# A new table of turns for a hybrid decoder layer: the same instructions in another order on every engine

## The chip, the cores and the metric

The kernel runs on one core of one Trainium2 chip. The core has a matrix engine (TensorE, PE in the profile; its weight loads are shown apart, as PEld), a vector engine (VectorE, DVE), an engine for activation functions (ScalarE, ACT), a general one (GpSimd, POOL), and SyncE (SP), whose queue issues the transfers between memory and SBUF. Each engine carries out its instructions in the order in which they stand in its queue, and engines wait for one another by semaphores. The metric is the time of one execution in microseconds of device time, as the median over runs. The kernel before took 839.03 us (three runs, 837.23 to 841.96).

## The reference

One layer of a decoder with 1024 tokens of width 1024, all in fp32. Cut to its steps:

```python
h = rms_norm(x, attn_norm_w)
a_q, a_k, a_v, a_z, a_b, a_a, b_q, b_k, b_v, b_z, i_q, i_k, i_w = split(h @ w_in)
# A: gated DeltaNet, 4 heads of 128, in chunks
qkv = silu(causal_dwconv(concat(a_q, a_k, a_v), conv_w))        # 4 taps
o_a = rms_norm(gated_delta_rule_chunked(q, k, v, g, beta)) * silu(a_z)
#   per chunk: v_new = val - kcd @ S; o = qd @ S + att @ v_new; S = S * gl + kd^T @ v_new
# B: sparse attention, 8 heads of 64 over 2 heads of keys and values
score = sum_h i_w[h] * relu(i_q[h] . i_k)                       # indexer, causal
o_b = softmax(b_q . b_k over the 256 keys of highest score) @ b_v * silu(b_z)
x = x + concat(o_a, o_b) @ w_out
x = x + (p @ w_ple) * sigmoid(rms_norm(x) @ w_gate + b_gate)
```

## The kernel before, in words

Tokens or channels lie on the 128 partitions, and matrices are worked in tiles of 128 x 512. An fp32 product is made of three matmuls in the type fp32r: each weight tile `raww` is loaded, rounded on ACT to `hiw` (L578), and the rest `low` is formed on POOL (L580); PE then multiplies high by high, low by high and high by low (`mm3`, L754). There are two buffers for `raww` and four each for `hiw` and `low`, so a weight tile's load waits until POOL has done with the one two before.

The work in rough order: RMSNorm, the per-layer embedding product (`start`, L772, with `pled` written out to memory for later); the indexer's products and scores (`logits`, L1047); the projections of four DeltaNet heads, each with a convolution of three taps on DVE (`tap`, L1237, which writes `acc` and `accq`); the inverse of a triangular matrix per chunk (`ftmp`, `Ub`, `Bb`); the recurrence (`gdn_s2`, L1358); the search for the 256th score of each row; attention; the output product; and the gate stage at the end.

The recurrence of one head has eight chunks. In each, PE multiplies the state S (into `rec`), DVE makes r from it, PE multiplies r by U, DVE makes `vnew`, PE multiplies `vnew` by `kh`, and DVE makes the next S from that. Other work of PE fills the time between these steps. Heads are counted from 0.

The search for the threshold is a bisection. For the last three blocks of 128 rows it runs on ACT (`junka` counts) and POOL (`nt`, `upa`), and ends with `va`. Then `topk_mask` (L1071) masks each block's row in two pieces on DVE: compare (`eq`), running count (`cum`), and two more passes, after which ACT writes the mask into `score`. The attention's keys `kst`, values `vst` and queries `Qt` are loaded into buffers that lie where the search's were (L1734 to L1750); ACT and DVE split Qt into the high and low part `qT`. PE makes the score products `S` from `kst` and `qT`.

In the gate stage (L1954 on) an output tile goes through: product on PE, DVE's scaling (`gth<-mm,rb`), ACT's sigmoid, DVE's product with the embedding (`gth<-gth,pld`), the sum with x, and the transfer out. `pld` has two buffers, `gth` two, and the tiles of the second half of the tokens are eight, the last of them cut into two pieces of 256 columns.

All engine calls are first recorded, 7513 of them with the marks of buffers, and each knows what it depends on. `Plan.run` (L457) then unpacks the text `TURNS` (L75) into one order of all records and `Plan.issue` (L506) issues them in it; an engine's queue holds its own calls in that order. Since L526 issues everything, every row of the profile has this line, and one reads it by the names of the tiles. A transfer, too, has its place in SP's queue by this table.

Of the kernel before, what the change touches and what calls it, by code (L numbers as in the profile page):

```python
# [2062 lines left out]
```

## Time and profile before

| | |
|---|---|
| runs | 837.23, 839.03, 841.96 us; median 839.03 |
| profiled execution | 838.3 us, span 836.6 us, mean granted clock of PE 0.995 |
| PE busy | 822.1 us, 98% of the span, 5171 matmuls |
| PEld, DVE, ACT, POOL busy | 698.3, 600.2, 562.1, 484.5 us |
| DMA | 97.34 MB at a mean of 116 GB/s |

The span is the time from the first to the last instruction of one profiled execution; some time lies around it. An engine row of the timeline has start, duration, engine, line, operation, the tile written and those read, their shapes, the count of instructions that are put together in it and, in brackets, how long the engine stood idle before and what ended that. SPq is the issuing of transfers. A transfer's row tells when it was issued, and its landing is seen in who waited for it.

### The profile page before, as it was taken

How to read it: one execution, taken by the hardware profiler on the slowest of the kernel's cores; microseconds unless marked ns; L12 is line 12 of the kernel's file. 1: busy time of each engine (PE TensorE's matmuls, PEld its weight loads, DVE VectorE, ACT ScalarE, POOL GpSimd, SP SyncE). 2: the span in 40 equal slices, each digit the busy share in tenths (PEclk: the TensorE clock that was granted, in tenths of full speed). 3: DMA queues.
4: the chain of work that ended last, by engine and by line, in shares of the span. 5: the costliest groups of instructions: out<-in, count | busy, mean ns of one | idle time of the engine just before them, and what ended most of it. 6: DMA issues, size and time to landing. Idle time of an engine off the chain costs nothing.

```text
span 836.6 us, 14789 instructions
## 1 busy us (share of the span) xinstructions
PE 822.1 (98%) x5171; PEld 698.3 (83%) x5171; DVE 600.2 (72%) x1369; ACT 562.1 (67%) x1285; POOL 484.5 (58%) x652
## 2 busy tenths in 40 slices
PE   8999999999999999989999999999999999999997
PEld 6898889988888888878888888777888888888876
DVE  3672536669488988899999978697776778452645
ACT  6663565555559889968999974688765767555432
POOL 3443433242159386775667786467864667768861
PEclk9999999999999999999999999999999999999999
DMA  8953221311212232222223223547435331345454
GB/s 291 372 182 118 65 76 51 83 64 45 78 40 64 52 100 69 70 70 93 78 56 83 85 97 126 180 161 240 153 99 157 96 101 39 126 161 190 124 180 139
DMA packets 80171, 97.34 MB, mean 116 GB/s; under 512 B 24256, under 2 KB 40928, under 8 KB 79968
## 3 DMA queue, kind: packets, MB, share of 16 engines
q1 hardware_dynamic: 80096, 96.40, 36.0%
q8 instruction: 40, 0.66, 0.3%
q14 instruction: 35, 0.29, 0.1%
HBM read 70.92 MB, written 25.45 MB: 115 GB/s over the span
## 4 chain that ended last, share of the span: by engine, by line
PE 82%; DVE 7%; DMA 6%; ACT 2%; issue 1%; POOL 1%; SPq 1%; DVEq 0%; POOLq 0%; ACTq 0%
PE mm L526 57%; PE s L526 6%; PE lg L526 6%; PE S L526 3%; PE pv L526 3%; PE pt L526 3%; PE rec L526 2%; PE po L526 2%; DVE eq L526 1%; DMA xt<-in_x_dram 1%; DVE gth L526 1%; SPq L526 1%; DVE P L526 1%; DMA raww<-in_w_ple_dram 1%; DMA dN<-NB 1%
## 5 line engine op out<-in xcount | busy, mean ns | idle before, releaser
L526 POOL TENSOR_TENSOR low<-raww,hiw 128x512 fp32r<-128x512 f32 (+1 forms) x135 | 183.4, 1365 | 166.3 <-ACT hiw L526 149.1
L526 PE MATMUL mm<-hTlo,hiw 128*128 128x512 f32 (+1 forms) x528 | 198.5, 386 | 0.0
L526 PE MATMUL mm<-hThi,hiw 128*128 128x512 f32 (+1 forms) x528 | 197.1, 385 | 0.0
L526 PE MATMUL mm<-hThi,low 128*128 128x512 f32 (+1 forms) x528 | 196.8, 386 | 0.0
L526 ACT ACTIVATE hiw<-raww 128x512 fp32r<-128x512 f32 x133 | 82.8, 627 | 69.5 <-PE mm L526 23.2
L526 PEld LDWEIGHTS mm<-hThi,low 128*128 128x128 f32 x528 | 99.8, 190 | 16.3
L526 PEld LDWEIGHTS mm<-hTlo,hiw 128*128 128x128 f32 x528 | 99.4, 189 | 16.0
L526 PEld LDWEIGHTS mm<-hThi,hiw 128*128 128x128 f32 x528 | 99.3, 189 | 15.6
L526 ACT ACTIVATE junka<-score,nt 128x768 bf16<-128x768 int16 (+5 forms) x96 | 99.8, 1040 | 3.8 <-POOL nt L526 1.3
L526 POOL TENSOR_SCALAR P<-P,rsum 128x128 f32<-128x128 f32 (+7 forms) x64 | 50.4, 798 | 41.9 <-DVE rsum L526 37.1
L526 ACT ACTIVATE relu<-lg 128x384 f32<-128x384 f32 (+3 forms) x80 | 40.4, 523 | 48.4 <-PE lg L526 42.4
L526 DVE TENSOR_SCALAR_CACHE_REDUCE junk<-score,cand 128x384 bf16<-128x384 f32 (+2 forms) x96 | 71.1, 740 | 1.5
L526 DVE SCALAR_TENSOR_TENSOR score<-relu,sm,score 128x384 f32<-128x384 f32 (+5 forms) x42 | 43.6, 1046 | 20.8 <-ACT relu L526 19.9
L526 ACT ACTIVATE ph<-pt 128x512 fp32r<-128x512 f32 x72 | 41.0, 594 | 24.7 <-PE pt L526 22.7
L526 ACT ACTIVATE P<-P,mn 128x128 f32<-128x128 f32 (+7 forms) x64 | 49.3, 771 | 12.0 <-DVE mn L526 10.7
L526 POOL TENSOR_SCALAR nt<-acca,upa 128x1 f32<-128x1 f32 x96 | 37.5, 393 | 33.1 <-ACT junka L526 30.2
L526 PE MATMUL S<-kst,qT 128*128 128x384 f32 (+4 forms) x192 | 53.8, 354 | 2.2 <-DMA kst<-kd 1.9
L526 DVE TENSOR_TENSOR pl<-pt,ph 128x512 fp32r<-128x512 f32 x72 | 47.8, 685 | 10.9 <-ACT ph L526 10.4
L526 PE MATMUL mm<-mcl,hiw 128*128 128x512 f32 x128 | 49.4, 396 | 0.0
L526 DVE SCALAR_TENSOR_TENSOR acc<-fst,cw,acc 128x512 f32<-128x512 f32 x48 | 38.7, 808 | 14.6 <-ACT acc L526 13.5
L526 PE MATMUL mm<-mch,hiw 128*128 128x512 f32 x128 | 49.1, 397 | 0.0
L526 PE MATMUL mm<-mch,low 128*128 128x512 f32 x128 | 48.9, 394 | 0.0
(296 smaller groups left out, 2066.4 us busy)
## 6 DMA issues: line engine op xcount, KB each, us to landing
raww<-in_w_ct_dram SPq DMA_DIRECT2D x66, 256.0 KB, 3.1
raww<-in_w_out_dram SPq DMA_DIRECT2D x32, 256.0 KB, 3.1
raww<-in_w_gate_dram SPq DMA_DIRECT2D x32, 256.0 KB, 2.5
xt<-in_x_dram SPq DMA_DIRECT2D x8, 512.0 KB, 8.2
...
```

The costliest lines, as they stand in the source:

```text
L526: r = getattr(getattr(self.nc, o.eng), fn)(*[real(x) for x in args], **{k: real(v) for k, v in kw.items()})
```

## The change

The text `TURNS` is replaced by another of the same length in records. No call, tile, pool or dependence is changed, and every engine issues the same instructions. The 5171 matmuls of PE are 3981 records (some hold several small ones), and 3545 of these have another place (10.6 places away in the mean, 236 at most); on DVE 983 of 1174 have (4.9 in the mean), on ACT 873 of 1015 (5.2), on POOL 547 of 648 (4.9), and of the transfers on SP 291 of 394 (3.2, at most 60). The diff is 68 lines of packed text, whose rows tell a reader nothing, so one stands for all:

```diff
 TURNS = r"""
-c-rlG32;=`neJV?@9n$yU3%X)^&+XImRei4b_t;s2@oIwTF`2-*nrI<_8lRx*@BIU4H)s_g&1suA;w|K#*UrXabA+CdP&M}GMUV
...
+c-rlm2XqzpmH(&DyqPyMZ|3#ht6tGl?*d7v_ksjM6d@!;FOsn77R8ic0mcSlFrpgA!3Kgc7~Eomo!DO68#}hMiIWq@$!0hFeg2!
...
 """
```

The first place is the step from chunk 3 to chunk 4 in the recurrence of head 1. On PE, before, from the product of `vnew` with `kh` to the next product with S (buffer numbers follow the names):

```order
L526 MATMUL rec_2474<-vnew_2565,kh_2459 128x128
L526 MATMUL po_2564<-S_2581,accq_2404 128x128
L526 MATMUL po_2564<-vnew_2454,att_2572 128x128
L526 MATMUL po_2564<-S_2455,accq_2404 128x128
L526 MATMUL s_926<-accq_849,acc_0_865 128x128
L526 MATMUL s_955<-ident_104,accq_849 128x128
L526 MATMUL po_2564<-vnew_2565,att_2572 128x128
L526 MATMUL rec_2474<-S_2570,acc_0_1297 128x128
```

and now, from the same product on:

```order
L526 MATMUL rec_2461<-vnew_2618,kh_2465 128x128
L526 MATMUL mm_148<-hTlo_248,hiw_145 128x512
L526 MATMUL mm_143<-hThi_244,hiw_125 128x512
L526 MATMUL mm_143<-hTlo_248,hiw_125 128x512
L526 MATMUL mm_143<-hThi_244,low_144 128x512
L526 MATMUL mm_148<-hThi_244,low_154 128x512
```

Rows of this kind, of 512 columns, go on up to `rec<-S,acc`, which is the 42nd row behind the first one here; before, it was the seventh. On DVE, before, the last taps of the convolution, two steps of the inverse's sums, and S:

```order
L526 SCALAR_TENSOR_TENSOR acc_0_840<-fst_225,cw_528,acc_0_840 128x512 x3
L526 TENSOR_TENSOR ftmp_841<-Ub_1087,Bb_1086 128x8x12
L526 SCALAR_TENSOR_TENSOR acc_0_840<-fst_224,cw_528,acc_0_840 128x512 x2
L526 TENSOR_REDUCE Ub_1087<-ftmp_841 128x8
L526 TENSOR_TENSOR ftmp_841<-Ub_1087,Bb_1086 128x8x13
L526 SCALAR_TENSOR_TENSOR S_2570<-S_2455,egl_842,rec_2474 128x128
L526 TENSOR_REDUCE Ub_1087<-ftmp_841 128x8
```

and now, from the `vnew` of that step to S:

```order
L526 TENSOR_SCALAR vnew_2618<-rec_2461,br_2598 128x128
L526 SCALAR_TENSOR_TENSOR acc_0_841<-fst_115,cw_684,acc_0_841 128x512
L526 SCALAR_TENSOR_TENSOR acc_0_841<-fst_114,cw_684,acc_0_841 128x512
L526 SCALAR_TENSOR_TENSOR acc_0_841<-fst_115,cw_684,acc_0_841 128x512
L526 TENSOR_TENSOR att_1379<-s_1064,scr_861 128x512
L526 SCALAR_TENSOR_TENSOR acc_0_841<-fst_114,cw_684,acc_0_841 128x512
L526 TENSOR_SCALAR junk_2407,acc_2408<-score_947,cand_0_2629 128x384
L526 SCALAR_TENSOR_TENSOR acc_0_841<-fst_114,cw_684,acc_0_841 128x512
L526 SCALAR_TENSOR_TENSOR acc_0_841<-fst_115,cw_684,acc_0_841 128x512
L526 SCALAR_TENSOR_TENSOR S_2621<-S_2433,egl_768,rec_2461 128x128
```

The taps (`acc<-fst,cw,acc`) stand ahead of S in both; the inverse's sums (`ftmp`, `Ub`) now come behind S.

The second place is the end of the recurrence of head 3 and the first loads of the attention. On DVE, before, from the last r of head 3 through its last `vnew` into the masks of the fourth to last piece:

```order
L526 SCALAR_TENSOR_TENSOR r_2571<-rec_2474,neg_eg_924,v_2607 128x128
L526 TENSOR_SCALAR vnew_2565<-rec_2474,br_2586 128x128
L526 TENSOR_SCALAR eq_2625<-score_927,va_2631 128x448
L526 SCALAR_TENSOR_TENSOR cum_2407<-eq_2625 128x448
L526 SCALAR_TENSOR_TENSOR eq_2625<-cum_2407,neda_2731,eq_2625 128x448
L526 SCALAR_TENSOR_TENSOR eq_2625<-score_927,va_2631,eq_2625 128x448
L526 SCALAR_TENSOR_TENSOR z_2614<-s_926,wa_213,z_2614 128x512
```

and now, from the `vnew` of the last chunk but two to the last one:

```order
L526 TENSOR_SCALAR vnew_2618<-rec_2461,br_2598 128x128
L526 TENSOR_SCALAR eq_2668<-score_947,va_2672 128x448
L526 SCALAR_TENSOR_TENSOR S_2623<-S_2621,egl_768,rec_2461 128x128
L526 SCALAR_TENSOR_TENSOR z_2652<-s_1057,wa_80,z_2652 128x512
L526 SCALAR_TENSOR_TENSOR r_2434<-rec_2461,neg_eg_778,v_2650 128x128
L526 TENSOR_SCALAR vnew_2432<-rec_2461,br_2598 128x128
L526 SCALAR_TENSOR_TENSOR cum_2381<-eq_2668 128x448
L526 SCALAR_TENSOR_TENSOR S_2433<-S_2623,egl_768,rec_2461 128x128
L526 SCALAR_TENSOR_TENSOR eq_2668<-cum_2381,neda_2850,eq_2668 128x448
L526 SCALAR_TENSOR_TENSOR r_2622<-rec_2461,neg_eg_778,v_2650 128x128
L526 SCALAR_TENSOR_TENSOR eq_2668<-score_947,va_2672,eq_2668 128x448
L526 TENSOR_SCALAR vnew_2618<-rec_2461,br_2598 128x128
```

The first piece with 448 columns and one z are now done between the steps of the recurrence. On SP, the transfers of the attention before:

```order
L526 DMA mixd<-z_2582 128x512
L526 DMA mixd<-z_2614 128x512
L526 DMA Qt_5438<-qd 128x4x128
L526 DMA raww_114<-in_w_ct_dram 128x512
L526 DMA Qt_5437<-qd 128x4x128
L526 DMA kst_5432<-kd 128x4x128 x2
L526 DMA vst_5574<-vd 128x2048
```

and now:

```order
L526 DMA mixd<-z_2624 128x512
L526 DMA mixd<-z_2652 128x512
L526 DMA kst_5443<-kd 128x4x128
L526 DMA raww_122<-in_w_ct_dram 128x512
L526 DMA Qt_5463<-qd 128x4x128
L526 DMA kst_5443<-kd 128x4x128 x2
L526 DMA Qt_5464<-qd 128x4x128
```

The first load of `kst` now stands ahead of both loads of `Qt`, and a load of weights stands between `kst` and the first `Qt`.

The third place is the end of SP's queue, in the gate stage. Before (the last four pairs of gate weights are rows of `raww`, an output is `out_dram`):

```order
L526 DMA out_dram<-gth_5933 128x512
L526 DMA raww_115<-in_w_gate_dram 128x512
L526 DMA raww_114<-in_w_gate_dram 128x512
L526 DMA out_dram<-gth_5841 128x512
L526 DMA raww_115<-in_w_gate_dram 128x512
L526 DMA pld_5929<-pled 128x512
L526 DMA pld_5908<-pled 128x512
L526 DMA out_dram<-gth_5933 128x512
L526 DMA pld_5929<-pled 128x512
```

and now:

```order
L526 DMA out_dram<-gth_5899 128x512
L526 DMA pld_5886<-pled 128x512
L526 DMA raww_124<-in_w_gate_dram 128x512
L526 DMA raww_122<-in_w_gate_dram 128x512
L526 DMA pld_5889<-pled 128x512
L526 DMA out_dram<-gth_5882 128x512
L526 DMA raww_124<-in_w_gate_dram 128x512
L526 DMA raww_122<-in_w_gate_dram 128x512
L526 DMA pld_5886<-pled 128x512
L526 DMA out_dram<-gth_5899 128x512
L526 DMA raww_124<-in_w_gate_dram 128x512
L526 DMA pld_5889<-pled 128x512
```

The load of `pld` for the sixth output tile was the sixth row of the first of these pieces, behind three tiles of weights; it is the fifth of the second, ahead of the last three tiles of weights. An output and a `pld` load now stand ahead of each pair of weights.

More of the change, by code (lines that the diff above doesn't have):

```diff
@@ new lines @@
+5|ah+*E8U%%gb?{5$!yPzsuU0YoEP9E|ZX|Z3OKAja$Lu$|nUK6TBklJbG<w#muvbDOj93AY$iJJbSQ;#%vk@WbH;#XbyX=%B+NRIMuTYKOR5<!KsWH3-tf(K*
+%rAwD8m*WAr8VLsBd5_0~MBMIBDCBmxMFL@8Q(Jo{g0^+Ioo+YW^m}{?fk2U~9<O&e;nL(4p98TY@w8}KM8TF8EeYFW;cyt6Z*@2vsoHIRz;3t0D`j?Pfx}T;>
+?<nrISL92y!rVKm%|bDWoG((PG@?;>5e)4hzap}-Tukfyk4(TTO|+*Ih`)Vg_dabML>>Gk09ElF3Xaz=+o29W^*JGO*0z|dc7O-$}XpK+BB^J(E810z19fm3@M
+Tdru1~9F>XjR6bCSWp&o`pAJA*Pm?oL-iMydO>Cv?KeX_w|17y8k))_y;YPITQs4fQo91gu*!DKR7EEc_9z}*;+VYr~t*d{S+OeR?pL{U_W$t0g1z|_2gz^gTP
+0B=jONkLM6YPDXY(XG)qolZ&8eugaRQ2L>V5EaY8>l~;49EM@asfvmUhEXxZfnnkRMQJFC;wc5@PAH0$WtmhkHP2NoB}tYg$=i2l&*uIW24f@D(l*RavV3q6qb
@@ new lines @@
+ez(qhuOD<^hptin3&Kib_RMvBE-?O63aYD3ES<e}6wg(_Bms1mmzW92<eq^y%Tyz4sbbg82B-_3y?~#F_uAriDIQcvmQgl^9AL!r@|33>FlmmT)jDD>pYcFHcM
+)vV(z4h3%7M4xQK`R7Y12ZLd;jXlS@SuvV+n+0d{AaJ%bV?x4q8nZmPa)27XvH}6z1!7OX6T{9fZN;*1I%mzw&gjut6=1_ipV^>k#QElJCg$vt!z7;E0NVI_<2
+w{&)SGx<tFyB4v?gK1orobs8gB9n@nR5?N@VI#P?1c*#F8#V^xToj*`HO4UuHD#kuIC$1J@wSZix)4!BDiqjo8SB<Z_VQV5hhVq>!s`0t%I+<X8ZZiPoL%&DGU
+t_jf{-&1IK}(iFYQ>o;~~0*%K$uoC$@lUmqGCdcyPi>#u(Rwx$dQp$hTOUBccu^YYs-zx?u>Z@%%t2Ooa;;Ts=)H1D(uXP=I;PM7nIx88co>2kdxy*54$r|-Qt
+{_gi*{qVaVFcS0VTW`Jp{^ea`FYf)m=7A5nPd<6;moL5ak|clY+rn!P0Y7?3b-=*vH*dLk3Fa6~Lx1JX8#g}rME*AXRDHHcKYHbrSI#|u?%efrH_yHQ{`)s>d<
@@ new lines @@
+Xb|B%!3Y-xdDlUxdGU=e_r?zWe;mn>U%Yp6sUm)DC(Wd+O>nwVJ#6?2QYrTz&SVn?HPR<ds*hU%htz{4+1VeC31Zo_q1d=U#XL_j7{RD?I+xlaF6K$LY@VyjFN
+j;mVtDzImQF`Xm73ZMELGapS3zXH}2gIH6ElsnT3ObM4GG&YU^%_=!^|E}uDb>C)A!S5H3r=){SMXP$ZH`t|F_uU$KS9G;!{`-#8%yGxgU31=t&_HS?9I(eb#{
+P~IFPd<71^5t(ldf|zQW9QF*_?uIwPED{!`yOE*gQ;ZMlSjtKF@}+j7*D7T8V#7ON@8pWcaA-D>C#xAV6|@DwslWl-sl6{_Uzg7;)`(DHhOK8VIG;7m^iiM<o!
+Q7!92Z5*eF2#>+ieo*s){x{ndsyH^2S%+wX1Ix^?S@gGQ6V!-vEB){lgT4yYd8{nMZB-nVaP{n*fzE7#ZU8M=CPX!ovt?*K5_9}W-icxHIyYpktz-n>=8mBGaF
+<y*IY{p%}MtXi>h<yo*jI5}}*c;(8~t52*|SiXGu;lpcI+;h+J;o%2YuG}}i=8@H_S6;bt<<P{lYgVpWLDS2ZE`8uZnq53PN{fkwLOgzQ!GilI1_l=N4-Am~M;
@@ new lines @@
+9D9GO=+ZsK>hAfq{G056oY?Y=}EPHg<W{(?tJS@^5CJ>7Bg?>}jdOwrvzeE9@T~-8*_enA&^~rKr(IKisfo!-fs*?d>h=M^o%->*~5+VK>my(qgqnS2O}Umn=~
+<1kN^ZhVj`+?%2`N(r~o7xuId(wi74X+S(dgK>!-Y$HyC5zq$6|3ym#}jZICB`|sJeZy(4W*|NH>d1qbS;lqa;TAQ0kYlw{-vAwnHH*Ffw>#g2|USBp9$4g6{C
+Afl|mj|w@Ksn9I%Brm$1hQ(fva++YYf|X-cruxhot=@Dl~GofQIsr9Vk!|+geosDBc4pg;|chCB9VB!@&8G&zy51&G#-srO|5)%Qug8pOG|$e&(Dv?_wJ3CmhQ
+`e+6v?GUGePb{TbO{$Op1sd+oJvN8|B$I*4iv6bGj<E)X6a4TqUPD1>juqR|Zm?d>I^9tu3C8z-G4h;LgzdBA7mDYwODb5In^n`RiE=Z!3@)4?B*k@-SqrfRBo
+00eRR^y%H*-LrZK{M@;4B*KG=%~?jYhcJp%i<y;uedGE-ZeO3Gf+L!8>*}d2p|ax)W>Hs^mC3Xt2PALV;9zerkMVtd-~_9BB<+AcfjumXl8R35Z652vjJ_4OZZ
@@ new lines @@
+;OF<XSAN878x^kYzL~MsT`ZPPaEvR51_EX1fdycgX8@J6tZoo@L+Z_3CYIx8EP|+d>}0I(IB)uoX%RZDC!BMX*?+Q8gOxr)Gk$U_tp=zZfx@%_hhvHDX9~fv@1
+2nsi>V-sWx%+1P-<*V}ypxC4ekR1%1?An5IO%EmYIJWU&u`T3L}81f6S<;(MyL!ep(syfHzvDh3AtNmU}(2}1oK?GSXRaMcj0Ktpc?IlyIC`z(gWvy8&8>Pa=M
+oGW4zO%D)F6g`}k%@>=wGf&@21_`ulg!Ad%TNovx~c|p-imUT<EHSEEJ<vonkXP7nNYbiGH8n>&%v5`J`?-`olR%aOa^!*da4%kDPs0)h!BW;A{6p?yj*KWW=4
+iT$>nkL5Qj_cbP56_LVNb4r?;92!VqHX_eC-?a2nQQp3?Lb(7I(KBO|P=R<n?VBbXox)`fyBYvm<^pczy?2P}YQ@tRJZUZ;D4mq-Lrlbo8H#T6h*mNT>1qZZWd
+*@v(!jfUey!Ne)bS5{W0Vn?^8sIJ~7;To9ZwG1=mYfx)5&T$-#5Cpmi#k81`WR~}(Xux`x^!DN?ig#C6%<Qk~T7aU{agxAWyHEn{=ztp#f#EnxkOWa(gJA?Y4Z
+}zrr)h?Uo4L8gg&8P{B{DLwB$^IyGHeBd(`YCJ&%zDJ3!JFgj9PD_T(aBk1{dPMWe?&;5W{Vh%?ABv*lc>e1weR{Np{0i9ETuA6T>0~L4_cs$3syrL;!)m{eeO
```

110 lines of the change are left out of this document (42 added, 68 removed).

## The prediction

> **What bounds the kernel now.** I read the page's busy shares first, then the chain that ended last (one piece of it stands below), then PE's waits, then the busy time stretch by stretch, and last the timeline around each stop.
>
> ```profile
> span 836.6 us, 14789 instructions
> PE 822.1 (98%) x5171; PEld 698.3 (83%) x5171; DVE 600.2 (72%) x1369; ACT 562.1 (67%) x1285; POOL 484.5 (58%) x652
> 429.60 11.62 PE mm L526 x51
> PE rec L526 <- DVE S L526: 2.5, 1, 2.5
> PE S L526 <- DMA kst<-kd: 1.9, 1, 1.9
> PE xT L526 <- DVE ident L526: 1.4, 1, 1.4
> 350.00:500.00 150.00, 147.53 (x1224) 126.34 (x1224) 137.20 (x375) 128.51 (x316) 104.85 (x211) 0.99 0.25 77
> 650.00:813.00 163.00, 163.00 (x796) 134.56 (x795) 100.47 (x186) 95.17 (x170) 117.01 (x90) 1.00 0.38 124
> ```
>
> TensorE is the bound: 98% busy, at 228 ns from one 512-column matmul to the next (11.62 us for 51). The change leaves all its matmuls in place, so nothing below the 822 us of busy time is in reach, and the granted clock is already 0.99 and 1.00 in these stretches. What an order can win is PE's idle time: 836.6 - 822.1 = 14.5 us in the span. 1.4 lie before the first matmul and 6.1 behind the last (part 3). The rows of the windows (start and end in us, length, then busy time of PE, PEld, DVE, ACT, POOL, PE's clock, DMA share and GB/s) and PE's waits say where most of the rest sits: 2.5 between 350 and 500, all in one stop, 1.9 at one load, nothing from 650 to 813. So two stops and the tail carry the sum.
>
> **Part 1: the state of head 1 in the recurrence (before: 357.4 to 360.2).**
>
> ```profile
> 357.39 0.39 PE L526 MATMUL po<-vnew,att 128*128 128x128 f32 x2
> 360.24 0.80 PE L526 MATMUL rec<-S,acc 128*128 128x128 f32 x2 [2.47 <-DVE S L526]
> 353.53 2.32 DVE L526 SCALAR_TENSOR_TENSOR acc<-fst,cw,acc 128x512 f32<-128x512 f32 x3
> 356.01 2.60 DVE L526 SCALAR_TENSOR_TENSOR acc<-fst,cw,acc 128x512 f32<-128x512 f32 x2
> 358.81 1.12 DVE L526 TENSOR_TENSOR ftmp<-Ub,Bb 128x104 f32<-128x104 f32 x1
> 359.86 0.33 DVE L526 SCALAR_TENSOR_TENSOR S<-S,egl,rec 128x128 f32<-128x128 f32 x1
> 356.79 2.94 POOL L526 TENSOR_TENSOR low<-raww,hiw 128x512 fp32r<-128x512 f32 x2
> 356.79 1.82 DVE acc L526
> ```
>
> PE has six short matmuls between the one that feeds S (vnew,kh) and the one that reads it, 1.4 us of work; DVE has the convolution taps, a step of the inverse's sums and then S in its queue. Two of the taps and the `ftmp` product were long (1.82 and 1.12 us; the three taps before took 2.32 together, 0.77 each) while POOL ran two `low` subtractions. In the new order the taps still stand ahead of S on DVE, but between the same two matmuls PE has 41 rows, nearly all 512 columns wide: 41 x 0.228 = 9.3 us. DVE's queue from vnew to S is six taps (6 x 0.77 = 4.6), one count and one product (about 1.4 more): 6 us, and 8 if two taps stretch again. It fits. **The stop of 2.5 us goes: -2.5.** Bounds: 0 (something else stops PE here) and -3.5 (the short matmuls after the restart run together instead of starting one by one).
>
> [...]
>
> **Part 2: the first keys of the attention (before: 527.2 to 529.5).**
>
> ```profile
> 527.20 0.39 PE L526 MATMUL mm<-hThi,hiw 128*128 128x512 f32 x1
> 529.49 0.36 PE L526 MATMUL S<-kst,qT 128*128 128x256 f32 x1 [1.90 <-DMA kst<-kd]
> 524.25 1.25 SPq L526 DMA_DIRECT2D kst<-kd  x2
> 523.79 0.37 SPq L526 DMA_DIRECT2D Qt<-qd  x1
> 527.75 1.93 ACT L526 ACTIVATE qT<-Qt 64x512 fp32r<-64x512 f32 x3 [0.30 <-DMA Qt<-qd]
> 528.47 1.58 DVE L526 TENSOR_TENSOR qT<-Qt,qT 64x512 fp32r<-64x512 f32 x2 [2.05 <-ACT qT L526]
> 493.55 0.42 DVE L526 TENSOR_SCALAR eq<-score,va 128x384 bf16<-128x384 f32 x1 [0.82 <-POOL va L526]
> 506.22 0.35 DVE L526 TENSOR_SCALAR vnew<-rec,br 128x128 f32<-128x128 f32 x1 [0.78 <-PE rec L526]
> 506.49 0.44 DVE L526 TENSOR_SCALAR eq<-score,va 128x448 bf16<-128x448 f32 x1
> 509.49 0.75 DVE L526 SCALAR_TENSOR_TENSOR z<-s,wa,z 128x512 f32<-128x512 f32 x1
> 523.01 0.75 DVE L526 SCALAR_TENSOR_TENSOR eq<-cum,neda,eq 128x512 bf16<-128x512 f32 x1
> 523.79 0.75 DVE L526 SCALAR_TENSOR_TENSOR eq<-score,va,eq 128x512 bf16<-128x512 f32 x1
> ```
>
> The row of waits names the load of keys, but two things came together there: the keys landed at about 529.4, and qT, which needs the load of Qt and then ACT and DVE, had its first half at 528.47 + 0.8 = 529.3. The Qt load went out at 523.79, the moment the last read of `cum` ended (523.01 + 0.75), since it takes over that buffer; kst stood behind it on SP. So the last masks of the selection set both. They are one block of DVE work: from the last vnew of head 3 (506.22) to 524.54, 18 us without a stop.
>
> In the new order one mask piece (506.49 to 509.49: 3.0 us) and one z (0.75) are done earlier, between the last steps of head 3, where DVE waited for PE anyway (the 0.78 at 506.22 is one of seven such waits from 496 on, 0.3 to 0.8 each). That leaves 18.3 - 3.8 = 14.5 us after that vnew. kst now goes out ahead of Qt and no longer counts; the first qT still needs Qt: 0.78 before the masks' end, 3.96 to land (523.79 to 527.75), one of ACT's three in 1.93 (0.64) and 0.8 on DVE give 4.6 after it, so S can start 19.1 us after the vnew. PE gets there after 91 rows where it had 100: (527.2 + 0.2 - 506.6) x 0.91 = 18.9. **The wait shrinks from 1.9 to a few tenths; I take -1.4**, with bounds of -1.9 and +1.5: if PE comes 2.5 sooner by part 1 and the masks do not, all of that turns up here.
>
> Do they come sooner? They begin with `va`, the end of the search on ACT and POOL, at 493.55.
>
> ```profile
> 362.79 0.63 ACT L526 ACTIVATE fst<-acc 128x512 f32<-128x512 f32 x1 [2.50 <-DVE acc L526]
> 440.00:480.00 40.00, 40.00 (x435) 33.95 (x434) 37.33 (x109) 38.06 (x94) 29.48 (x65) 1.00 0.28 86
> ```
>
> Right after the stop of part 1 ACT stood waiting 2.50 us for the same taps, and from 440 to 480 it was busy 38.06 of 40. Work that starts earlier behind that stop is handed on, so I expect most of the 2.5 us to reach `va`. It is the weakest link of the sum.
>
> **Part 3: the tail.**
>
> ```profile
> 820.94 1.74 SPq L526 DMA_DIRECT2D pld<-pled  x2
> 815.20 1.06 DVE L526 SCALAR_TENSOR_TENSOR gth<-gth,pld 128x512 f32<-128x512 f32 x1 [0.79 <-ACT gth L526]
> 824.73 1.82 DVE L526 SCALAR_TENSOR_TENSOR gth<-gth,pld 128x512 f32<-128x512 f32 x1 [1.20 <-ACT hiw L526]
> 830.13 0.42 DVE L526 TENSOR_TENSOR gth<-mm,rb 128x256 f32<-128x256 f32 x1
> 831.93 0.42 DVE L526 TENSOR_TENSOR gth<-mm,rb 128x256 f32<-128x256 f32 x1
> 830.22 0.28 PE L526 MATMUL mm<-h1Bh,low 128*128 128x256 f32 x1
> ```
>
> PE ends at 830.5, but DVE takes up the last half tile at 831.93, because the first half came at 830.13 out of a backlog: the sixth tile's product with pld ran only at 824.73, its load having stood on SP behind a pair of gate weights until 820.94. Its buffer was free at 815.20 + 1.06. In the new order that load goes ahead of the last three tiles of weights. Without the backlog the first half is taken up when PE has it: 16 matmuls of 0.12 us (256 columns) before the last, 830.22 - 1.9 + 0.28 = 828.6, and the second at PE's end, 830.5 instead of 831.9. What follows stays as it is. **-1.3**, bounds 0 and -1.5.
>
> **Part 4: what gets tighter.** At the head DVE sets four tables before `ident`, so the warming transposes start about 0.5 us later than 1.45; PE then meets the same loads of the first weights, so +0.1 (0 to +0.6). In the recurrence of head 2, in two places DVE has 6 to 7 us queued against 8 to 11 of PE's work, and the attention has more places where a probability tile is wanted within 0.3 us of being ready. The nearest rows are the short waits between DVE and PE above, such as the 0.78: **+0.6**, bounds 0 and +3 (one stop like part 1's).
>
> Sum: -2.5 - 1.4 - 1.3 + 0.1 + 0.6 = -4.5. The profiled execution took 838.3, its span being 836.6 with 1.7 around it; it gives 833.8. The median of the runs shown, 839.03, is 0.7 above that execution, so I forecast **834.5 us**.
>
> **The rivals.** About 0.5%, 4.2 us, is what a measurement of this kernel can tell from no change.
>
> First, the masks do not come sooner. `va` stays at 493.55; from there DVE has 31.0 us to 524.54, with 4.2 us of waits for PE in it. If the waits stay, S starts at 529.3 and parts 1 and 2 together give 0.2 instead of 3.9: 834.5 + 3.7 = 838.2. For it: the search runs on two engines that PE does not feed. Against: ACT's waits after 360, and the piece that fills DVE's waits.
>
> Second, slower: weights behind outputs in the gate stage. The new SP order puts each pair of gate weights behind an output and a pld load; before, weights mostly went first.
>
> ```profile
> 804.57 1.29 DVE L526 TENSOR_TENSOR gth<-mm,rb 128x512 f32<-128x512 f32 x2 [4.69 <-PE mm L526]
> 810.50 0.34 SPq L526 DMA_DIRECT2D out_dram<-gth  x1
> 804.65 0.33 SPq L526 DMA_DIRECT2D raww<-in_w_gate_dram  x1
> 807.20 0.63 ACT L526 ACTIVATE hiw<-raww 128x512 fp32r<-128x512 f32 x1 [0.66 <-DMA raww<-in_w_gate_dram]
> ```
>
> The second output of this half went out at 810.50. Weights issued 0.4 behind it, 2.6 to land (804.65 to 807.20 for those that this row of ACT waits for) and 0.63 on ACT, would be ready at 814.1, and their `low` part 1.5 later (half of part 1's 2.94); PE wants them 19.6 us before its end, counted in its new order at 0.228 and 0.12 us a matmul, so at about 810.9 and 811.4: 4 us lost, and again at the next pairs. With two such stops and no gain in the tail: 834.5 + 1.3 + 8 = 843.8. It decides if that output goes out after about 808. Against it: 810.50 was late because DVE took the third tile's product ahead of the second's (the pair at 804.57); now the second stands first, PE ends it 31.1 us before its own end, at 799.7, and the output can go at about 803.5.
>
> Third, the stretch moves. Part 1's stop needed two long taps; other places now have little room, and a chance meeting of DVE and POOL costs about 1 us each. If one takes back part 1's gain: 834.5 + 2.5 = 837.0. [...]
>
> **How the numbers follow.** Forecast 0.52, masks 0.22, stretch 0.13, weights 0.13. Around the forecast I allow 831 to 837.5, for the bounds of parts 2 and 4. Two thirds of it lies below 834.8, which with a few chances from beyond gives faster 0.43; the rest of it, the masks and the stretch give same 0.44; the weights slower 0.13. The range that holds 8 in 10 reaches from 830.0 to 841.5.
>
> **What would show it.** The wait for S in head 1 is gone from PE's waits; PE's wait at the first keys is under 0.7 us and starts 2 to 3 us earlier than 527.2; `va` comes at about 491; from PE's last matmul to the end of the span it is 5 us, not 6.4; PE stays whole from 650 to the end. Wrong if PE shows a new stop above 1.5 us in the recurrence of heads 2 and 3, or any stop on hiw or low behind 800.

## The result, and the profile after

The changed kernel took 826.40 us (median of four runs, 825.72 to 826.98) beside 838.93 us (four runs, 837.23 to 841.96): a ratio of 0.985, 95% interval 0.982 to 0.988. It is faster by 12.5 us where 4.5 were forecast, and below the range of 830.0 to 841.5. So the direction was right and the size 2.8 times too small.

From the page of the changed kernel its span and the busy time; then PE's waits, all of them (engine, tile, what it waited for: us in all, times, longest):

```profile
span 824.7 us, 14808 instructions
PE 815.3 (99%) x5171; PEld 695.8 (84%) x5171; DVE 596.6 (72%) x1369; ACT 558.6 (68%) x1285; POOL 472.7 (57%) x652
PE xT L526 <- DVE ident L526: 2.1, 1, 2.1
PE mm L526 <- ACT plt L526: 1.0, 1, 1.0
PE mm L526 <- ACT hiw L526: 0.5, 1, 0.5
PE mm L526 <- DVE plo L526: 0.4, 1, 0.4
PE pt L526 <- DVE pl L526: 0.3, 1, 0.3
```

Both long stops are gone, and with them three of the four short ones in the attention; at the head the wait for `ident` is longer (2.1, before 1.4) and one of 1.0 for `plt` is new. But the row of engines holds the surprise: PE's busy time, which the prediction took for a floor, fell by 6.8 us, from 822.1 to 815.3, with the same 5171 matmuls. Not only PE's waiting got shorter; its work did.

The span shrank by 836.6 - 824.7 = 11.9 us. Where it went is read by comparing the times at which PE starts its matmuls at the same amount of its own work done (columns multiplied, so that the order does not matter much; a border between two rows is uncertain by up to 0.4 us, since it can fall among matmuls of another length). What each stretch gained, with the forecast (minus is a loss):

| stretch of the old run, us | gained, us | forecast |
|---|---|---|
| 0 to 340, head and first projections | 0.6 | -0.1 |
| 340 to 400, the stop at head 1's state | 4.5 | 2.5 |
| 400 to 520 | 0.2 | 0 |
| 520 to 540, the first keys | 3.6 | 1.4 |
| 540 to 640, attention | 1.4 | -0.6 (for the recurrence and attention together) |
| 640 to the last matmul | 0.3 | 0 |
| behind the last matmul | 1.4 | 1.3 |

Two rows stand out: at each of the two stops 1.7 to 2 us more came back than the stop had lasted. And the head and the attention gained where a loss was forecast.

**Where the extra came from.** Windows of the kernel before, of 1 or 2 us, behind the two stops (start and end, length, busy time and instructions of PE, PEld, DVE, ACT, POOL, then PE's granted clock, DMA share, GB/s):

```profile
360.00:361.00 1.00, 0.76 (x4) 0.76 (x4) 0.95 (x3) 0.28 (x3) 0.81 (x2) 0.55 0.00 0
361.00:362.00 1.00, 1.00 (x5) 0.81 (x4) 0.93 (x2) 0.00 (x0) 1.00 (x1) 0.50 0.20 74
364.00:366.00 2.00, 2.00 (x10) 1.62 (x9) 2.00 (x4) 0.53 (x2) 1.30 (x1) 1.00 0.24 90
531.00:532.00 1.00, 1.00 (x5) 0.81 (x5) 0.74 (x3) 0.88 (x4) 0.00 (x0) 0.50 1.00 346
```

The granted clock is the column behind POOL's. Behind each stop it is 0.50 for 3.41 us, from 360.10 and from 530.76, and then 1.00 again. Of PE's timeline of the same run, the matmuls there:

```profile
361.48 0.63 PE L526 MATMUL mm<-hThi,low 128*128 128x512 f32 x1
364.27 0.39 PE L526 MATMUL mm<-hTlo,hiw 128*128 128x512 f32 x1
```

A 512-column matmul takes 0.63 us there instead of 0.39, and the next follows 0.42 us later instead of 0.23. All that time counts as busy: two stretches of 3.41 us at half clock hold 1.7 us too much each, 3.4 of the 6.8 us by which the busy time fell. The other 3.4 are spread, and no run shows their cause. In the window of 150 us that the prediction quoted the same stretch reads 0.99: 1% of 150 us is 1.5 us, and the prediction passed it over. The same row of the changed kernel, and the one from 650:

```profile
350.00:500.00 150.00, 149.93 (x1245) 128.85 (x1244) 136.55 (x381) 131.26 (x332) 105.67 (x218) 1.00 0.27 81
650.00:813.00 163.00, 163.00 (x783) 134.53 (x783) 102.19 (x178) 92.89 (x164) 116.39 (x91) 1.00 0.43 133
```

PE is whole in both, at full clock, where before it stood for 2.5 us of the first.

After, the same places. From DVE's and PE's timelines of the changed kernel at head 1's state:

```profile
350.21 1.63 DVE L526 SCALAR_TENSOR_TENSOR acc<-fst,cw,acc 128x512 f32<-128x512 f32 x1
352.30 1.41 DVE L526 SCALAR_TENSOR_TENSOR acc<-fst,cw,acc 128x512 f32<-128x512 f32 x2
353.63 0.34 DVE L526 SCALAR_TENSOR_TENSOR S<-S,egl,rec 128x128 f32<-128x128 f32 x1
357.73 0.39 PE L526 MATMUL rec<-S,acc 128*128 128x128 f32 x2
```

S is ready at 353.97 and used at 357.73: 3.8 us to spare. The last two taps took 1.41 together; before, they had taken 2.60. But the tap ahead of them was long here (1.63, beside a `low` of POOL at 350.00), so the meeting of taps and `low` is not gone: PE's 41 rows now last longer than DVE's queue with a long tap in it. At the first keys (DVE, SP, DVE, PE):

```profile
487.84 0.42 DVE L526 TENSOR_SCALAR eq<-score,va 128x384 bf16<-128x384 f32 x1 [0.46 <-POOL va L526]
502.07 0.35 DVE L526 TENSOR_SCALAR vnew<-rec,br 128x128 f32<-128x128 f32 x1 [0.19 <-PE rec L526]
515.34 0.37 SPq L526 DMA_DIRECT2D Qt<-qd  x1
519.60 1.40 DVE L526 TENSOR_TENSOR qT<-Qt,qT 64x512 fp32r<-64x512 f32 x2 [3.23 <-ACT qT L526]
521.39 0.40 PE L526 MATMUL S<-kst,qT 128*128 128x256 f32 x2
```

`va` comes 5.7 us earlier than before (487.84 against 493.55), the load of Qt 13.3 us behind head 3's last vnew where it was 17.6, and the first half of qT at about 520.3, a good 1 us before PE wants it.

### The profile page after: what moved, and what is told of

Read it like the earlier page. It is cut to its first block, busy times and chain, and to the rows that moved or that the text cites. A ratio compares the mean times of both kernels' runs of the same rounds, so it can differ in the third digit from the quotient of the medians.

```text
span 824.7 us, 14808 instructions
## 1 busy us (share of the span) xinstructions
PE 815.3 (99%) x5171; PEld 695.8 (84%) x5171; DVE 596.6 (72%) x1369; ACT 558.6 (68%) x1285; POOL 472.7 (57%) x652
## 4 chain that ended last, share of the span: by engine, by line
PE 92%; DMA 4%; ACT 2%; DVE 1%; SPq 1%; issue 0%; ACTq 0%
PE mm L526 64%; PE s L526 6%; PE lg L526 6%; PE pv L526 4%; PE S L526 4%; PE pt L526 4%; PE rec L526 3%; PE po L526 2%; DMA pled<-plt 2%; DMA xt<-in_x_dram 1%; DMA zd<-fst 1%; DMA xt<-in_pT_dram 1%; SPq L526 1%; ACT P L526 1%; ACT plt L526 0%
## 5 line engine op out<-in xcount | busy, mean ns | idle before, releaser
L526 POOL TENSOR_TENSOR low<-raww,hiw 128x512 fp32r<-128x512 f32 (+1 forms) x135 | 181.3, 1348 | 168.4 <-ACT hiw L526 164.6
L526 PE MATMUL mm<-hThi,low 128*128 128x512 f32 (+1 forms) x528 | 194.3, 381 | 0.0
L526 ACT ACTIVATE relu<-lg 128x512 f32<-128x512 f32 (+3 forms) x80 | 40.0, 523 | 44.1 <-PE lg L526 41.5
L526 POOL TENSOR_SCALAR nt<-acca,upa 128x1 f32<-128x1 f32 x96 | 39.3, 412 | 33.1 <-ACT junka L526 31.7
L526 ACT ACTIVATE fst<-mm 128x512 f32<-128x512 f32 (+2 forms) x61 | 30.1, 506 | 22.5 <-PE mm L526 17.8
```

Source lines behind the costliest of these rows:

```text
L526: r = getattr(getattr(self.nc, o.eng), fn)(*[real(x) for x in args], **{k: real(v) for k, v in kw.items()})
```

## The experiments

A place in the table is named by the time at which PE is there. In each edit the records keep their dependences; only `TURNS` is written anew, or one line of `Plan.issue` as well. The diffs show the rows that move on an engine, without buffer numbers. Ratios are against the kernel before on the same chip, with 95% intervals.

**The new order up to a place, the old one behind it.** Four cuts, at 340, 372, 545 and 780 us:

```diff
-TURNS: the order of the kernel before
+TURNS: the new order up to the place; the rest of the records in their old order
```

> The new order up to the records that PE reaches at about 340 us of its span, and the old order for all that is left; nothing left out. Theory (a stop of PE costs its own length and then about 1.7 us more, because the granted clock is halved for some 3.4 us behind it): the stops at head 1's state and at the first keys are still there, so the span is within 1 us of the kernel before (-0.6). Rival 1 (the gain comes from fewer changes between long and short matmuls all over the program): a third of that has been collected by here, -1.5 to -2 us. Rival 2 (a stop costs only its own length): the same as the theory here.

> The new order up to about 372 us, that is past the step of head 1 at which PE stopped before, the old order behind it; nothing left out. Theory: the stop of 2.5 us and its slow stretch are gone, -4 to -5 us against the kernel before, if the wait at the first keys stays what it was. Rival 2 (only the stop's own length): -3. Rival 3 (PE comes sooner to the first keys, but the masks do not): the wait there grows from 1.9 to over 4 us and the total gain is under 1.5 us.

> The new order up to about 545 us, past the first keys of the attention, the old order behind it; nothing left out. Theory: a second step of about -3.6 us (1.9 of wait and 1.7 of slow clock), so -8.5 to -9 us against the kernel before. Rival 2 (only the stop's own length): -5.

> The new order up to about 780 us, the old order for the last part of the gate stage; nothing left out. Theory: the short stops of the attention are gone too, another -1.3, so about -10.5 us against the kernel before; what the whole change has beyond that (about -1.3) is the tail. Rival (the tail gives nothing of its own): -12, the same as the whole change.

| cut at | median, us | ratio |
|---|---|---|
| 340 | 835.98 (before 838.69) | 0.997 [0.996, 0.999] |
| 372 | 839.64 | 1.001 [1.000, 1.003] |
| 545 | 830.05 | 0.989 [0.985, 0.993] |
| 780 | 828.56 | 0.988 [0.986, 0.991] |

The cut at 545 has 8.6 of the 12.5 us and no wait for the keys; the cut at 780 10.1, although PE stood 2.1 us for `rs` at 30 us in its profiled run, with 3.41 us at half clock behind it. Most of the gain sits before 545, as the table of stretches says. The cut at 372 came out 5 to 6 us slower than forecast, and its total decides nothing: its profiled run gained 4.7 us on the old one at head 1 (from 356 to 366), as the theory has it, but where new and old order meet, PE stood 2.5 us for `sqj` and 1.7 us for W at 375 to 381, stops that neither whole table has, and then ran 6.83 us at half clock.

The wait for the first keys is in all five profiled runs that have the old order there (before, cut_340, cut_372, low_late, s_early: 1.9 to 2.5 us) and in none that has the new one.

The cut at 340 brought something else. Its order around the stop of head 1 is the old one, row for row, and still the stop is absent. From its timelines (DVE, DVE, POOL) and its waits of PE:

```profile
355.72 1.53 DVE L528 SCALAR_TENSOR_TENSOR acc<-fst,cw,acc 128x512 f32<-128x512 f32 x2
357.70 0.35 DVE L528 SCALAR_TENSOR_TENSOR S<-S,egl,rec 128x128 f32<-128x128 f32 x1
358.06 2.53 POOL L528 TENSOR_TENSOR low<-raww,hiw 128x512 fp32r<-128x512 f32 x2
PE S L528 <- DMA kst<-kd: 2.0, 1, 2.0
```

Here POOL's two `low` subtractions start at 358.06, behind the taps; before, they started at 356.79, in the midst of them. The taps took 1.53 instead of 2.60, and S came in time. DVE also stood 0.85 us further ahead of PE than before (see the table below). So the old order does not force the stop.

**The meeting alone.** Old table; one small instruction of POOL ahead of the `low` subtractions is given five times, so that they start later. It writes the same value each time.

```diff
+AGAIN = {3573: 5}
-            for fn, args, kw in o.parts:
+            for fn, args, kw in o.parts * AGAIN.get(o.i, 1):
```

> The old table; one small product of POOL (nt, ahead of the two low subtractions at 356.79 us) is done five times over, with the same result, so that POOL does more and the subtractions start 1 to 1.5 us later, behind the taps; nothing left out. Theory (the stop at head 1's state comes from the meeting of taps and low subtractions): the taps take 0.75 us each again, S is ready in time, PE's stop of 2.5 us there goes, -2.5 to -4 us against the kernel before. Rival (DVE is late there with or without POOL): the stop stays above 1.5 us and the time within 1 us of the kernel before.

Measured: 835.90 against 837.19, 0.998 [0.995, 1.001]: less than the 2.5 to 4 us forecast, and too little to tell from nothing by time alone. The timelines (POOL, POOL, DVE) and the wait of PE tell more:

```profile
356.11 3.08 POOL L529 TENSOR_SCALAR nt<-acca,upa 128x1 f32<-128x1 f32 x5 [0.24 <-ACT junka L529]
359.16 2.53 POOL L529 TENSOR_TENSOR low<-raww,hiw 128x512 fp32r<-128x512 f32 x2
356.58 1.54 DVE L529 SCALAR_TENSOR_TENSOR acc<-fst,cw,acc 128x512 f32<-128x512 f32 x2
PE rec L529 <- DVE S L529: 0.9, 1, 0.9
```

With `low` out of the way the taps took 1.54 and `ftmp` 0.34 (before: 2.60 and 1.12), and PE's stop shrank from 2.5 to 0.9. The clock stayed at 1.00 there, and between 356 and 400 PE gained 2.7 us on the old run. `low` now met the next tap, at 360.51 (1.73 us), where PE did not wait for it.

Four profiled runs have the same order at this place, and together they tell what the stop is made of. From the start of PE's product of vnew with kh to the product that reads S it is 1.45 us if nothing is waited for. DVE has to get from the start of its last pair of taps to S in that time, and in what it is ahead of PE at the start:

| run | pair of taps starts, against PE's product | from there to S ready, us | what met `low` | PE's stop, us |
|---|---|---|---|---|
| before | 0.15 ahead | 4.18 | a tap (1.82) and `ftmp` (1.12) | 2.47 |
| rev_460 (below) | 0.64 ahead | 3.36 | `ftmp` (1.37) | 1.16 |
| low_late | 0.16 behind | 2.33 | neither | 0.93 |
| cut_340 | 1.00 ahead | 2.33 | neither | none |

Each stop is the third column less 1.45 and less the lead, to about 0.1 us. So the meeting made 1.85 us of the 2.47 (4.18 - 2.33). The rest is the order, with six short matmuls of PE to cover DVE's queue, and how far ahead DVE happens to be, which differs by over 1 us among these runs.

**S ahead of the last tap.** The other half of part 1 by itself, in the old table. DVE's queue:

```diff
 TENSOR_TENSOR ftmp<-Ub,Bb 128x8x12
-SCALAR_TENSOR_TENSOR acc<-fst,cw,acc 128x512 x2
+SCALAR_TENSOR_TENSOR acc<-fst,cw,acc 128x512
+SCALAR_TENSOR_TENSOR S<-S,egl,rec 128x128
+SCALAR_TENSOR_TENSOR acc<-fst,cw,acc 128x512
 TENSOR_REDUCE Ub<-ftmp 128x8
 TENSOR_TENSOR ftmp<-Ub,Bb 128x8x13
-SCALAR_TENSOR_TENSOR S<-S,egl,rec 128x128
```

> The old table with one record moved: the state of head 1 after chunk 3 on DVE, from behind the last tap and the ftmp product to ahead of the last tap; nothing left out. Theory (stop plus slow clock behind it): PE's stop of 2.5 us goes and the clock stays whole there, about -4 us, if the wait at the first keys does not grow. Rival 2 (the stop's own length only): -2.5. Rival 3 (PE only waits longer for the first keys): 0 to -1, with a wait of 4 to 6 us there.

Measured: 839.05 against 837.99, 1.002 [1.000, 1.004]: no gain. Its timelines (DVE, DVE, DVE, PE):

```profile
357.65 0.34 DVE L527 SCALAR_TENSOR_TENSOR S<-S,egl,rec 128x128 f32<-128x128 f32 x1
357.91 1.69 DVE L527 SCALAR_TENSOR_TENSOR acc<-fst,cw,acc 128x512 f32<-128x512 f32 x1
359.80 1.12 DVE L527 TENSOR_TENSOR ftmp<-Ub,Bb 128x104 f32<-128x104 f32 x1
362.13 0.49 PE L527 MATMUL rec<-r,U 128*128 128x128 f32 x2 [2.37 <-DVE r L527]
```

S was ready in time, but the long tap and the long `ftmp` now stood ahead of r, and PE waited 2.37 us for that, at the next product of the recurrence. DVE's work had not become less. So S further up is not enough by itself; in the new order the 41 rows of other work that PE has there cover the queue, with 3.8 us to spare. No run has these 41 rows alone.

**The price of a stop.** To see what a stop of PE costs without changing any order, the new table was taken and four DVE products of the indexer's queries (`qlo`) were given several times over, so that PE waits for them at four places between 150 and 245 us. They repeat a result that is there already. A short version for stops of about 1 to 2 us, and a long one:

```diff
+AGAIN = {1643: 3, 1747: 4, 1493: 4, 2013: 5}      # short
+AGAIN = {1643: 7, 1747: 9, 1493: 7, 2013: 10}     # long
-            for fn, args, kw in o.parts:
+            for fn, args, kw in o.parts * AGAIN.get(o.i, 1):
```

> The new table; four products of DVE that PE waits for in the indexer's stage (low parts of q) are repeated 3, 4, 4 and 5 times, so that PE stands still there for about 0.5, 0.7, 1.3 and 1.7 us; the repeats write the same values again. Theory: each stop costs its length, and those above a bound between 1.3 and 1.9 us cost some 1.7 us more at half clock: against the new table +4 us if none is over the bound, +6 if the longest is. Rival (no slow clock, each costs its length): +4. Rival (every stop however short brings the slow clock): +10.

> As the run with short stops, but the four products repeated 7, 9, 7 and 10 times, so that PE stands still for about 1.9, 2.5, 3.2 and 4.8 us (12.4 in all); nothing left out. Theory: each is followed by about 3.4 us at half clock, 1.7 us lost, so +19 us against the new table. Rival (each costs its length): +12.4. Rival (the slow stretch grows with the stop): more than +20.

Measured: 832.58 and 848.93 us (0.995 [0.993, 0.997] and 1.014 [1.012, 1.016]). PE's waits of the short and the long version, then of the long one PE's first matmul behind its first stop, and a window behind it:

```profile
PE mm L530 <- DVE qlo L530: 3.5, 3, 2.1
PE lg L530 <- DVE qlo L530: 1.5, 1, 1.5
```

```profile
PE mm L530 <- DVE qlo L530: 11.3, 3, 5.7
PE lg L530 <- DVE qlo L530: 3.7, 1, 3.7
151.51 0.41 PE L530 MATMUL lg<-khi,qlo 128*128 128x320 f32 x1 [3.68 <-DVE qlo L530]
153.00:154.00 1.00, 1.00 (x4) 0.74 (x3) 0.77 (x2) 0.62 (x2) 0.62 (x1) 0.50 0.00 0
```

The profiled spans, 830.9 and 847.9, are 6.2 and 23.2 above the changed kernel's 824.7. In the short version the four stops took 5.0 us, and the clock stayed at 1.00 until PE's work was done: the stops are nearly the whole price, the longest of 2.1 us among them, for which the forecast had allowed half clock. In the long version the stops, longer than the 12.4 us planned, took 15.0, and 17.1 us ran at half clock, which is 8.5 more: 23.5 for the 23.2 measured. By stops alone it would have been 15.0. Note the clock at 151.5, when PE starts again: it is not yet low; the slow stretch begins at 152.56.

The slow stretches before the end of PE's work are 3.41 us long, or twice that, and they start on a grid of 3.413 us: in the kernel before at 360.10 and 530.76, 170.66 apart, 50 steps; in the long version at 152.56, 173.04, 196.93 and 241.31, 6, 7 and 13 steps apart. Where the grid lies differs from run to run: counted back in such steps, also from the start at 380.74 in rev_460 below, its first boundary in the span is at 1.7 us in the kernel before, 2.4 in the long version and 1.9 in rev_460. Whether a window of the grid was slow went, in most of the cases below, by how long PE stood idle in the window before it. The idle share here is the part of a grid window in which PE was not busy by the view of windows; where a stop reaches over a boundary, both windows are given:

| run, at | stop, us | idle share of a grid window | next window |
|---|---|---|---|
| before, 360 | 2.5 | 0.68 | half clock |
| before, 530 | 1.9 | 0.56 | half clock |
| s_early, 530 | 1.9 | 0.57 | half clock |
| cut_340, 527 | 2.0 | 0.58 | half clock |
| cut_780, 32 | 2.1 | 0.59 | half clock |
| long stops, four | 2.4 to 5.7 | 0.63 to 1.0 | half clock, once for two windows |
| cut_372, 533 | 2.5 | 0.53 and 0.20 | full |
| mask_late, 506 | 2.1 | 0.53 | full |
| s_early, 362 | 2.4 | 0.38 and 0.31 | full |
| low_late, 527 | 1.9 | 0.27 and 0.30 | full |
| short stops, 230 | 2.1 | 0.09 and 0.51 | full |
| rev_460, 7 | 0.7 and 0.2 | 0.33 | half clock |
| rev_460, 378 | 1.2 | 0.36 | half clock |
| rev_460, 468 | 0.4 and 1.1 | 0.42 | half clock |

Without the last three rows the border lies between 0.53 and 0.56. These do not fit: waits of hardly more than 1 us, or less, were followed by half clock. Of the one at 378 PE's row behind the wait, one of its next rows, and the next window of the grid:

```profile
378.57 0.49 PE L526 MATMUL rec<-S,acc 128*128 128x128 f32 x2 [1.21 <-DVE S L526]
379.09 0.73 PE L526 MATMUL s<-T,NB 32*32 32x16 f32 x64
380.74:384.15 3.41, 3.41 (x61) 2.99 (x50) 3.34 (x10) 3.41 (x13) 1.77 (x3) 0.50 0.02 5
```

What the three have in common was not tried. At 378 and 468 a good part of PE's busy time went to small matmuls (over 64 of 32*32, and 16 of 64*64), where the windows of all other rows hold 128*128 ones alone; at 7 there are seven single 512-column matmuls, whose rows last 0.4 to 0.5 us each where in a run one follows the other after 0.23. The busy time of the view may thus be more than what the clock goes by; that is the author's reading, and no run shows it. So the idle share by itself does not tell every case.

Still, in these runs a stop of 2.5 us that fell across a boundary of the grid went free, where one of 1.9 inside a window was followed by half clock, which is 1.7 us more. Two such stops of the same kind, at the first keys, in windows of two runs (the row of PE, then the window that holds the 3.5 us behind it): first of the cut at 372, then of s_early:

```profile
533.13 0.36 PE L528 MATMUL S<-kst,qT 128*128 128x256 f32 x1 [2.50 <-DMA kst<-kd]
533.00:537.00 4.00, 3.87 (x23) 3.42 (x24) 2.66 (x15) 1.72 (x9) 0.68 (x2) 1.00 0.97 341
```

```profile
530.70 0.36 PE L527 MATMUL S<-kst,qT 128*128 128x256 f32 x1 [1.93 <-DMA kst<-kd]
531.50:535.00 3.50, 3.50 (x13) 3.01 (x13) 2.26 (x11) 1.37 (x7) 0.33 (x1) 0.53 0.92 303
```

The longer stop left the clock at 1.00, the shorter one at 0.53. The place of the grid would also explain why the kernel before scatters by 4.7 us over its four runs and the changed one by 1.3: with two stops near this size, where the grid lies may decide each time whether they cost the extra; that is the author's estimate. The 56 runs of the kernel before that were timed beside these experiments bear it out in part. One slow window takes 0.002 off the mean clock of a run (half of 3.41 us in 837), and the five runs with a mean clock of 0.999 have a median of 835.9 us, the nine with 0.995 one of 839.2: 3.3 us for two windows at 1.7.

**The second part alone, taken back.** New table; the mask piece and z go back to behind the last vnew of head 3. DVE's queue:

```diff
 TENSOR_SCALAR vnew<-rec,br 128x128
-TENSOR_SCALAR eq<-score,va 128x448
 SCALAR_TENSOR_TENSOR S<-S,egl,rec 128x128
-SCALAR_TENSOR_TENSOR z<-s,wa,z 128x512
 ...
-SCALAR_TENSOR_TENSOR cum<-eq 128x448
 SCALAR_TENSOR_TENSOR S<-S,egl,rec 128x128
-SCALAR_TENSOR_TENSOR eq<-cum,neda,eq 128x448
 SCALAR_TENSOR_TENSOR r<-rec,neg_eg,v 128x128
-SCALAR_TENSOR_TENSOR eq<-score,va,eq 128x448
 TENSOR_SCALAR vnew<-rec,br 128x128
+TENSOR_SCALAR eq<-score,va 128x448
+SCALAR_TENSOR_TENSOR cum<-eq 128x448
+SCALAR_TENSOR_TENSOR eq<-cum,neda,eq 128x448
+SCALAR_TENSOR_TENSOR eq<-score,va,eq 128x448
+SCALAR_TENSOR_TENSOR z<-s,wa,z 128x512
```

> The new table with the first 448-column mask piece and one z on DVE moved back behind the last vnew of head 3, as they stood before; the kst load stays ahead of Qt; nothing left out. Theory: the masks end 3.8 us later, PE stands 3 to 3.5 us at the first keys, and the idle share of one 3.41 us stretch of the clock's grid is over 0.6, so 1.7 us of slow clock follow: +4.5 to +5 us against the new table's 826.4. Rival (the place of the masks does not matter, the load order does): under +1.

Measured: 829.67 against 837.73, 0.991 [0.989, 0.994], about 3.3 us of the gain lost where 4.5 to 5 were forecast. But PE did not wait at the keys. From the timelines of ACT and PE:

```profile
505.48 0.58 ACT L528 ACTIVATE score<-eq 128x448 f32<-128x448 bf16 x1 [4.59 <-DVE eq L528]
505.96 0.16 ACT L528 ACTIVATE fr<-mm 128x8 f32<-128x8 f32 x1
506.18 0.50 PE L528 MATMUL mm<-hThi,hiw 128*128 128x512 f32 x1 [2.11 <-ACT fr L528]
```

ACT's writing of the mask waits for the late `eq`, 4.59 us; `fr`, which only reads a product of PE out of PSUM, stands behind it in ACT's queue; and PE waits 2.11 us for the room that `fr` makes, with a second wait of 1.1 at 521. The clock stayed full (mean of that run 0.999). So the place of the mask pieces is worth 3.2 us of stops in the new table, and by a path that the prediction did not follow: what stands behind a waiting instruction on its own engine.

**Old order up to 460, new order behind.**

```diff
-TURNS: the order of the kernel before
+TURNS: the old order up to 460 us; the rest of the records in their new order
```

> The old order up to the records that PE reaches at 460 us, the new order behind it; nothing left out. Theory: the stop at head 1's state is left as it was, the one at the first keys, the short stops of the attention and the tail are as in the new order: -3.7 - 1.3 - 1.3, so -6 to -7 us against the kernel before. Rival (the new order of the masks only works because everything before it is earlier too): a wait of 1 us and more at the first keys, and -3 or less.

Measured: 836.53 against 837.19, 0.999 [0.998, 1.001], where -6 to -7 us were forecast: as a sum, inconclusive. In the profiled run 1.7 us were lost at half clock already at 8.69, in the old order. At head 1 the stop was 1.16 instead of 2.47, without half clock behind it, but the wait of 1.21 at 378 and its slow window took that back. Where the two orders meet, between 460 and 480, PE waits 0.4 for `o` and 1.1 for T and then runs a window at half clock: 3 us. Behind it, from 480 to 560, this run gains about 4 us on the old one, without a wait for the keys, and some 1.5 more by 640. That agrees with the 3.6 and 1.4 of the whole change there.

**The tail.** New table; two loads of `pld` go back behind the weights and an output on SP:

```diff
 DMA raww<-in_w_gate_dram 128x512
-DMA pld<-pled 128x512
 DMA out_dram<-gth 128x512
 ...
 DMA raww<-in_w_gate_dram 128x512
-DMA pld<-pled 128x512
 DMA out_dram<-gth 128x512
 ...
 DMA pld<-pled 128x512
+DMA pld<-pled 128x512
+DMA pld<-pled 128x512
 DMA out_dram<-gth 128x512
```

> The new table with two SP transfers moved back: the pld loads of the sixth and seventh output tile behind the last tile of gate weights; nothing left out. Theory: DVE falls behind again at the end, +1 to +1.5 us against the new table's 826.4, with PE's last matmul where it was and the tail behind it 6.3 us instead of 5. Rival (the new order of the halves and of the products on DVE is what shortened the tail): under +0.4.

Measured: 826.99 against 837.73, 0.987 [0.985, 0.990]; from PE's last matmul to the end it took 5.14 us where the changed kernel takes 4.99 and the one before 6.4. The changed kernel's last rows of PE and DVE:

```profile
819.66 0.29 PE L526 MATMUL mm<-h1Bh,low 128*128 128x256 f32 x1
818.06 0.42 DVE L526 TENSOR_TENSOR gth<-mm,rb 128x256 f32<-128x256 f32 x1 [0.81 <-PE mm L526]
819.98 0.42 DVE L526 TENSOR_TENSOR gth<-mm,rb 128x256 f32<-128x256 f32 x1
```

DVE takes the first half up 1.6 us before PE's last matmul and the second 0.3 behind it, both as forecast. But the load's place on SP is not what did it: put back, it costs 0.15 us of the 1.4. The order of the last stage as a whole does it: the nine profiled runs that have the new one there unchanged take 4.99 to 5.01 us, the seven with the old one 5.29 to 6.50. Which of its moves makes the rest was not isolated.

**Two small ones.** In the new order PE changes from a run of short matmuls (up to 128 columns) to longer ones 151 times, before 190 times. A table with more such changes, by moving single 512-column matmuls into runs of short ones at 37 places between 245 and 780 us, one of them here:

```diff
 MATMUL rec<-S,acc 128x128
+MATMUL mm<-hThi,hiw 128x512
 MATMUL s<-acc 128x128
 ...
-MATMUL mm<-hThi,hiw 128x512
```

> The new table with 52 long matmuls of PE moved forward into runs of short ones between 245 and 780 us, which makes 37 more changes between short and long, about as many as the old table had more; nothing left out. Theory: a change costs some 40 ns, +1.5 us against the new table's 826.4, spread evenly and with no wait. Rival 1 (a change costs nothing): within 0.4. Rival 2 (the short matmuls that come later make DVE and ACT late): over +3, with waits in the recurrence.

Measured: 827.98 us, 0.989 [0.986, 0.992], some 1.6 us above the changed kernel's 826.4, which was timed on another occasion, with no new wait of PE; its profiled span, 825.0, is 0.3 above. If the difference is that of the changes, one costs by this estimate about 8 to 43 ns (0.3 and 1.6 us over 37), and the 39 that the new table saves are worth 0.3 to 1.7 us. That is too wide to call it measured.

And one that might have been better still: the changed kernel stands 0.97 us at 33 us for `plt`, so on ACT that instruction goes ahead of the sums of squares.

```diff
 ACTIVATE plt<-mm 128x512
-ACTIVATE sq,ss<-xt 128x1024
 ACTIVATE plt<-mm 128x512
+ACTIVATE sq,ss<-xt 128x1024
```

> The new table with one ACT record moved: the copy of an embedding product (plt, at 32.35 us) goes ahead of the sum of squares that waits for x at 31.29; nothing left out. Theory: PE's stop of 1.1 us at 31.6 goes, -0.8 to -1.1 us against the new table's 826.4 (about 825.5). Rival (the sum of squares is later by 0.6 and PE waits for the normalised x instead): within 0.3 of 826.4.

Measured: 824.95 against 837.73, 0.986 [0.983, 0.988]. To see whether these 1.4 us are real, it was run again beside the changed kernel on one chip:

> The new table once more, beside plt_again on the same chip, to set the two against each other. Every theory: 826 to 827 us.

> The new table with the one ACT record (plt) moved ahead of the sum of squares, once more. Theory: PE's stop of 1.1 us at 31.6 is gone and half of it is kept: 0.5 to 1.4 us under new_again. Rival (the first look was chance): within 0.3 of it.

Measured: 825.73 us for the changed kernel (0.988 [0.986, 0.990]) and 826.02 for the edit (0.988 [0.986, 0.990]). There is no difference, and in that run 0.4 us of the wait for `plt` remained. It is no better version.

## Why the prediction was wrong in size

**The step that failed** is the first: "nothing below the 822 us of busy time is in reach, and the granted clock is already 0.99 and 1.00 in these stretches". A matmul at half clock counts as busy (0.63 us for 512 columns at 361.48, 0.39 at full clock), so the floor was not one, and a mean over 150 us hid 3.4 us at 0.50. What the runs showed in its place: each of the two stops cost its own length and 1.7 us more. That is 3.4 of the 8.1 us between the forecast of 834.5 and the 826.4 measured. A second step failed by almost as much: the term of part 4, +0.7 in the forecast and -2.5 measured, had the wrong sign, and what made it is in part open. Some 0.8 us are what parts 1 and 2 gained beyond stop and clock, and 0.7 the allowance for the median, which the changed kernel did not need (its profiled execution took 826.38).

**Part 1** had the mechanism right: the 41 rows cover DVE's queue, and S comes with 3.8 us to spare. Forecast -2.5, measured -4.5; with the half clock the sum is 2.47 + 1.7 = 4.2. The bound of -3.5 was too near, since it allowed for the matmuls behind the restart only in their starting, not in their clock. Of the pair of taps only one was long (1.82 of the 2.60), not two. And part of the 2.5 was luck of that one execution: the same order gave stops of 1.16, 0.93 and none in other profiled runs.

**Part 2** was right in its path and too careful in its size: -1.4 forecast, -3.6 measured, which is the 1.9 of the wait and 1.7 of half clock. Qt went out 13.3 us behind the last vnew, where 13.7 had been worked out (14.5 less 0.78); `va`, "the weakest link", came at 487.84 instead of about 491, so no wait was left at all. What the mask pieces hold up when they are late, though, is ACT's queue first and the keys only then, as mask_late shows.

**Part 3** was right in size (-1.4 against -1.3). That the order of the last stage makes it is shown, the named cause is not: taken back, the load costs 0.15.

**Part 4** had the wrong sign. Forecast were +0.1 for the head and +0.6 for what gets tighter; measured, these stretches gained 2.5 us. The first matmul comes 0.6 later, as said, but this is made up by 20 us, and so is the new wait of 1.0 for `plt` by 340. In the recurrence and the attention no new wait appears. The attention gained 1.4, of which 0.9 are waits of PE: four of 0.2 to 0.4 before, one of 0.3 after. The other 1.6 us are spread thin over these stretches; the saved changes of length may be a part of it, at a price the runs do not settle, and what makes the rest stays open.

**The rivals.** The masks did come sooner, so the first fell. Weights behind outputs stopped nothing: PE has no wait behind 650. (The 799.7 in that rival should be 799.4, 830.5 less 31.1, which changes nothing.) Of the third, the meetings of DVE and POOL are real and made 1.85 us of part 1's stop. Taps (`acc<-fst,cw,acc`) of more than 1.5 us are two in each kernel: 1.78 and 1.82 us at 152 and 357 before, 1.68 and 1.63 at 76 and 350 after. But no stop of PE followed, since there was work enough to cover them.
